# Two hybrid attention layers in float32 on one core: the broadcast of the forget logs through a scratch in device memory, issued by GpSimd

## The chip, the cores and the metric

The kernel runs on one core of a Trainium2 chip. A core has five engines that run their own instruction streams and meet at semaphores: TensorE (PE, matmuls; its weight loads are listed as PEld), VectorE (DVE), ScalarE (ACT), GpSimd (POOL) and SyncE (SP), which here does nothing but issue DMAs. Sixteen DMA engines move data between device memory and the on-chip memory SBUF, which has 128 partitions. Matmuls write to banks of a second on-chip memory, PSUM. The metric is device time of one execution in microseconds (us); lower is better.

## The reference

Two identical layers work on `x` of 512 tokens by 1024 channels. Each layer normalises and modulates `x`, projects it, and feeds three branches of four heads each: retention, gated linear attention (GLA) and forgetting attention ("fox"). The branches are gated, mixed and added to `x`; a gated feed-forward block with a short causal convolution follows. The branch that the change touches is this one:

```python
def forgetting_attention(q, k, v, f_logit):
    log_f = jax.nn.log_sigmoid(f_logit.astype(F32))
    cum = jnp.cumsum(log_f, axis=1).transpose(0, 2, 1)          # one row of 512 per head
    for blk in range(s // Q_BLOCK):                              # 128 queries at a time
        q0, q1 = blk * Q_BLOCK, (blk + 1) * Q_BLOCK
        logits = jnp.einsum('bihd,bjhd->bhij', q[:, q0:q1], k[:, :q1]) * d ** -0.5
        logits = logits + cum[:, :, q0:q1, None] - cum[:, :, None, :q1]
        ...
        p = jax.nn.softmax(jnp.where(mask, logits, -jnp.inf), axis=-1)
        outs.append(jnp.einsum('bhij,bjhe->bihe', p, v[:, :q1]))
```

In each logit the cumulated log of the query's position is added and that of the key's position subtracted. With queries on the partitions, the first is one number per partition, and the second is a row of 512 numbers that every partition needs.

## The kernel before

**Weights and matmuls.** All weights lie in device memory as `wall`, cut into 302 units of 128 x 1024 floats (512 KB) in the order of their use. A unit is loaded into a raw tile `wr` by SyncE (`dma_to`, L114; four buffers), copied by ScalarE into a rounded part `wh` (`prep_hi`, L122), and VectorE subtracts the two into the remainder `wl` (`prep_lo`, L131), which also frees the raw tile. Each product is made of three matmuls (high by high, high by low, low by high). `col_block` (L239 to L241) makes 128 channels by 512 tokens from one unit; `tok_group` (L534 to L536) makes token-major tiles from several units. `ahead` prepares units in advance of the one in use, four deep in the part that matters here.

**The order of the work.** The program order is written by hand, and every engine executes its own instructions in that order. SyncE's queue holds weight loads, tables and, before the change, the broadcasts. Beside the big matmuls, small pieces of the three branches ("items") are written as generators. `tick`, called within each block of matmuls, lets waiting items take a step: a step of kind "e" emits work of VectorE, ScalarE and GpSimd, a step of kind "p" emits matmuls, if enough of the three PSUM banks of the pool `psa` are free. An item that follows takes its turn from a queue with spacings written in the program.

**Around the change.** After the values of the fox branch (`fv`) come the projections of GLA's queries and keys; with the keys come the forget logits. `gk_evac` then queues `gates_item`, two `la_item` (the GLA decays), and sixteen `fox_item`, head by head and four query blocks each. Meanwhile TensorE makes GLA's values (`gv`, a `tok_group` of four units), then retention's queries (`rq`).

`gates_item` transposes the logits, forms the log-sigmoid, and VectorE's scan (L589) leaves `cum` with one head's 512 numbers in each of partitions 0 to 3. TensorE transposes it into `cumc` (L593), the per-query numbers. Then each head's row is broadcast into a tile `cumb` of 128 x 512 by a DMA (L597).

A `fox_item` multiplies queries and keys (`fs`, L649), after which VectorE forms the logits with `cumc` and `cumb` (L653), masks them and takes the maximum; ScalarE exponentiates (L658) and scales (L661); TensorE transposes the result (L665) and multiplies by the values (L675). An item may start only when its head's normalised queries and keys and the `cumb` tiles are there in the program's order. GpSimd, in this part of the program, has the multiplication in the normalisation of queries and keys (L492), before the gates, and the additions of the rotary embedding (L690), after GLA's values.

All [128, 512] tiles of float32 come from one pool of 59 slots, `cum` and `cumb` among them.

Of the kernel before, what the change touches and what calls it, by code (L numbers as in the profile page):

```python
# [7 lines left out]
F32 = mybir.dt.float32  # L8
# [17 lines left out]
S = 512  # L26
NH = 4
# [27 lines left out]
def tile_hybrid_layers(ctx: ExitStack, tc: tile.TileContext, xT, cvec, wall, wada, par, a2, cst, tabs, out):  # L55
# [5 lines left out]
    wh_p = ctx.enter_context(tc.tile_pool(name="wh", bufs=5))  # L61
    wl_p = ctx.enter_context(tc.tile_pool(name="wl", bufs=5))
    sm_p = ctx.enter_context(tc.tile_pool(name="sm", bufs=2))
    psm = ctx.enter_context(tc.tile_pool(name="psm", bufs=8 - NA, space=PS))
    psa = ctx.enter_context(tc.tile_pool(name="psa", bufs=NA, space=PS))

    V, A, G, T, Q = nc.vector, nc.scalar, nc.gpsimd, nc.tensor, nc.sync

    def slot(nm, dt=F32):
        return slots.tile([128, S], dt, tag="slot", name=nm)  # L70
# [6 lines left out]
    def free(n=1):  # L77
        live[0] -= n

    def ba(nm="ba"):  # L80
        live[0] += 1
        return psa.tile([128, S], F32, tag="a", name=nm)
# [3 lines left out]
    def cc(n):  # L86
        o, w = CC[n]
        return C[:, o:o + w]
# [3 lines left out]
    def pp(l, n, i=0, w=1):  # L92
        o, _ = PC[n]
        return P_l[l][:, o + i:o + i + w]
# [377 lines left out]
    def layer(l, nm, h):  # L472
# [80 lines left out]
        def gk_evac(b, o):  # L553
            if b == 0:
                R["gk"] = [slot("gk"), slot("gk")]
                R["sml"] = sm_p.tile([128, NB, 20], F32, tag="sml", name="sml")
            A.copy(R["gk"][b // 2][:, (b % 2) * 256:(b % 2) * 256 + 256], o[:, 0:256])
            V.tensor_copy(R["sml"][:, b, :], o[:, 256:276])
            if b == NB - 1:
                queue.append((gates_item(), 1))  # L560
                queue.append((la_item(0), 1))
                queue.append((la_item(1), 1))
                for hh in range(NH):
                    for ib in range(NB):
                        queue.append((fox_item(hh, ib), 1 + ib // 2))

        def gates_item():
            yield P1
            ps = ba("smT")
            for b in range(NB):  # L570
                T.transpose(ps[0:20, b * 128:b * 128 + 128], in_=R["sml"][:, b, :], identity=cc("ident"))
            yield E_
            gl = slot("glrT")
            V.memset(gl[0:32, :], 1.0)
            V.tensor_copy(gl[0:20, :], ps[0:20, :])
            free()
            e = slot("fe")
            m = slot("fm")
            fb = pp(l, "foxb")[0:4]
            A.activation(e[0:4], gl[0:4], AF.Abs, bias=fb)  # L580
            A.activation(e[0:4], e[0:4], AF.Exp, scale=-1.0)
            A.activation(e[0:4], e[0:4], AF.Ln, bias=cc("one")[0:4])
            V.tensor_scalar(m[0:4], gl[0:4], fb, 0.0, op0=ALU.add, op1=ALU.min)
            yield E_
            R["glrT"] = gl
            V.tensor_tensor(m[0:4], m[0:4], e[0:4], op=ALU.subtract)
            V.memset(e[0:4], 1.0)
            cum = slot("cum")
            V.tensor_tensor_scan(cum[0:4], e[0:4], m[0:4], 0.0, op0=ALU.mult, op1=ALU.add)  # L589
            yield P1  # L590
            pc = ba("cumc")
            for b in range(NB):
                T.transpose(pc[:, b * 4:b * 4 + 4], in_=cum[0:4, b * 128:b * 128 + 128],  # L593
                            identity=cc("ident")[0:4, 0:4])
            cb = [slot("cumb") for _ in range(NH)]
            for hh in range(NH):
                Q.dma_start(out=cb[hh], in_=cum[hh:hh + 1, None, :].to_broadcast([1, 128, S]))  # L597
            yield E_
            R["cumc"] = sm_p.tile([128, 16], F32, tag="cumc", name="cumc")
            V.tensor_copy(R["cumc"], pc[:, 0:16])  # L600
            free()
            R["cumb"] = cb
# [604 lines left out]
```

## Time and profile before

| | |
|---|---|
| Time, median of 3 runs | 1866.81 us (1865.39 to 1867.63) |
| Span of the profiled execution, first to last instruction | 1864.4 us (its time outside the span is not listed) |
| Matmuls | 8991 |
| DMA packets, data moved | 65395, 220.01 MB |
| DMA issues of the broadcasts | 8 (4 per layer), 256 KB written each |
| DMA issues of weight units | 302, 512 KB each |

How to read it: the profile lists each engine's busy time and its share of the span, then the span in 40 equal slices of 46.6 us, each with a digit for the busy tenth (9 is 90% or more). PEclk is the granted clock of TensorE in the same form. The chain of work goes back from the last instruction to what released it, step by step. A wait is put down to the event that came last. L numbers are lines of the kernel; `out<-in` gives the tiles' names; SPq is SyncE's queue. "us to landing" runs from a DMA's issue until its data have arrived.

### The profile page before, as it was taken

What the parts mean: (1) busy time and instruction counts of PE and PEld (TensorE: products, weight loads), DVE (VectorE), ACT (ScalarE), POOL (GpSimd) and SP (SyncE); (2) the same over time, 40 slices, a digit from 0 to 9 for tenths busy, and PEclk for the clock granted to TensorE, in tenths of its full rate; (3) what the DMA queues carried; (4) which work ended last, traced back from release to release, by engine and by line L of the source; (5) the groups of instructions that cost most, each with busy time, mean ns of one, the idle gap of its engine ahead of it and who ended that gap; (6) DMA issues with size and microseconds to landing.
All of it is one profiled execution on the core that took longest, in us unless ns stands there. A gap on an engine that the chain in (4) does not pass through costs nothing.

```text
span 1864.4 us, 22544 instructions
## 1 busy us (share of the span) xinstructions
PE 1805.6 (97%) x8991; PEld 1508.4 (81%) x8991; DVE 1002.1 (54%) x1515; ACT 672.2 (36%) x1124; POOL 85.4 (5%) x101
## 2 busy tenths in 40 slices
PE   9995999999999999999999869999999999999999
PEld 6874878888889888888898648788888898888887
DVE  7663754565665676764257347544434466444321
ACT  4662433332333443332148334333323244333210
POOL 3210100000000000000001001000000000000000
PEclk9997999999999999999999979999999999999999
DMA  9346222345552465554223542322222233322231
GB/s 335 126 55 92 69 91 90 125 158 192 169 181 86 152 236 181 191 193 158 79 69 124 38 98 69 102 91 69 90 95 98 79 102 102 100 93 94 71 121 55
DMA packets 65395, 220.01 MB, mean 118 GB/s; under 512 B 7263, under 2 KB 7689, under 8 KB 65290
## 3 DMA queue, kind: packets, MB, share of 16 engines
q1 hardware_dynamic: 65290, 218.57, 38.5%
q8 instruction: 71, 1.16, 0.3%
q14 instruction: 34, 0.28, 0.0%
HBM read 214.34 MB, written 2.10 MB: 116 GB/s over the span
## 4 chain that ended last, share of the span: by engine, by line
PE 92%; DMA 3%; DVE 2%; SPq 2%; ACT 1%; issue 0%; POOL 0%; DVEq 0%; ACTq 0%
PE bm L239 23%; PE bm L241 23%; PE bm L240 23%; PE bm L363 4%; PE ga L363 4%; PE bm L534 3%; DMA wr<-wall 3%; PE bm L535 2%; PE bm L536 2%; SPq L597 2%; PE ro L795 1%; PE rs L783 1%; PE fs L649 1%; PE fo L675 1%; PE go L761 0%; ACT wh L122 0%
## 5 line engine op out<-in xcount | busy, mean ns | idle before, releaser
L131 DVE TENSOR_TENSOR wl<-wr,wh 128x1024 fp32r<-128x1024 f32 x302 | 368.8, 1224 | 360.3 <-ACT wh L122 360.0
L239 PE MATMUL bm<-hhi,wh 128*128 128x512 f32 x1296 | 520.3, 401 | 0.0
L241 PE MATMUL bm<-hhi,wl 128*128 128x512 f32 x1296 | 505.5, 390 | 0.0
L240 PE MATMUL bm<-hlo,wh 128*128 128x512 f32 x1296 | 504.9, 390 | 0.0
L122 ACT CAST wh<-wr 128x1024 fp32r<-128x1024 f32 x302 | 314.5, 1047 | 358.5 <-PE bm L240 232.2
L239 PEld LDWEIGHTS bm<-hhi,wh 128*128 128x128 f32 x1296 | 243.4, 188 | 54.4 <-issue 4.2
L240 PEld LDWEIGHTS bm<-hlo,wh 128*128 128x128 f32 x1296 | 243.5, 188 | 53.0 <-issue 2.9
L241 PEld LDWEIGHTS bm<-hhi,wl 128*128 128x128 f32 x1296 | 243.2, 188 | 51.9
L239 PE MATMUL bm<-fah,wh 128*128 128x512 f32 (+1 forms) x374 | 141.0, 377 | 0.0
L240 PE MATMUL bm<-fal,wh 128*128 128x512 f32 (+1 forms) x374 | 140.8, 377 | 0.0
L241 PE MATMUL bm<-fah,wl 128*128 128x512 f32 (+1 forms) x374 | 140.8, 377 | 0.0
L534 PE MATMUL bm<-wh,hhi 128*128 128x512 f32 (+1 forms) x256 | 99.7, 389 | 0.0
L151 DVE SCALAR_TENSOR_TENSOR ar<-ar,cact 128x1024 f32<-128x1024 f32 x80 | 97.5, 1218 | 0.0
L535 PE MATMUL bm<-wl,hhi 128*128 128x512 f32 (+1 forms) x256 | 95.5, 373 | 0.0
L536 PE MATMUL bm<-wh,hlo 128*128 128x512 f32 (+1 forms) x256 | 95.1, 371 | 0.0
L240 PEld LDWEIGHTS bm<-fal,wh 128*128 128x128 f32 x374 | 70.3, 188 | 13.0
L241 PEld LDWEIGHTS bm<-fah,wl 128*128 128x128 f32 x374 | 70.3, 188 | 13.0
L239 PEld LDWEIGHTS bm<-fah,wh 128*128 128x128 f32 x374 | 70.3, 188 | 12.7
L904 DVE SCALAR_TENSOR_TENSOR x<-bm,mod,x 128x512 f32<-128x512 f32 (+1 forms) x39 | 25.5, 655 | 101.3 <-PE bm L241 101.3
L942 DVE TENSOR_TENSOR fu<-fu,bm 128x512 f32<-128x512 f32 x42 | 28.9, 688 | 69.6 <-PE bm L241 59.8
L867 ACT ACTIVATE mg<-bm,der 128x512 f32<-128x512 f32 x48 | 32.9, 685 | 82.4 <-PE bm L241 82.4
L941 ACT ACTIVATE fu<-fu 128x512 f32<-128x512 f32 x44 | 27.8, 632 | 93.9 <-DVE fu L939 93.9
(213 smaller groups left out, 2406.3 us busy)
## 6 DMA issues: line engine op xcount, KB each, us to landing
wr<-wall SPq DMA_DIRECT2D x302, 512.0 KB, 3.6
ar<-wada SPq DMA_DIRECT2D x80, 512.0 KB, 3.9
ad<-wada SPq DMA_DIRECT2D x32, 256.0 KB, 6.0
x<-xT SPq DMA_DIRECT2D x8, 256.0 KB, 4.2
cumb<-cum SPq DMA_DIRECT2D x8, 256.0 KB, 30.2
dec<-tabs SPq DMA_DIRECT2D x8, 256.0 KB, 4.3
out<-x SPq DMA_DIRECT2D x8, 256.0 KB, 2.1
cos<-tabs SPq DMA_DIRECT2D x2, 256.0 KB, 4.0
```

Source lines behind the costliest of these rows:

```text
L122: A.copy(hi, raw[i])
L131: V.tensor_tensor(lo, raw.pop(i), hi.bitcast(F32), op=ALU.subtract)
L151: V.scalar_tensor_tensor(out=r, in0=r, scalar=1.0, in1=cact, op0=ALU.mult, op1=ALU.mult, accum_out=mod[l][:, b:b + 1])
L239: T.matmul(o, lhsT=wh, rhs=ah, start=first, stop=False)
L240: T.matmul(o, lhsT=wh, rhs=al, start=False, stop=False)
L241: T.matmul(o, lhsT=wl, rhs=ah, start=False, stop=last)
L363: T.matmul(banks[f % GB][:, ts], lhsT=got[f // 8][wi][:, (f % 8) * 128:(f % 8) * 128 + 128], rhs=h[kc][hi][:, ts], start=kc == 0 and hf != ...
L534: T.matmul(o, lhsT=h[k][0][:, bs], rhs=wh[:, ws], start=k == 0, stop=False)
L535: T.matmul(o, lhsT=h[k][0][:, bs], rhs=wl[:, ws], start=False, stop=False)
L536: T.matmul(o, lhsT=h[k][1][:, bs], rhs=wh[:, ws], start=False, stop=k == KD - 1)
L597: Q.dma_start(out=cb[hh], in_=cum[hh:hh + 1, None, :].to_broadcast([1, 128, S]))
L867: A.activation(g, o, AF.Tanh, scale=0.5, bias=der[l][:, i * 8 + j:i * 8 + j + 1])
```

## The change

A pool of scratch tiles in device memory is added. In `gates_item`, GpSimd writes `cum` (four rows of 512 floats, 8 KB) into a scratch tile, and the four broadcasts read their row from the scratch in place of the SBUF tile. They are issued from GpSimd's queue in place of SyncE's. The destinations, the tiles' order and all other instructions stay as they were. The broadcasts depend on the write, so GpSimd issues them once the write has landed.

```diff
     sm_p = ctx.enter_context(tc.tile_pool(name="sm", bufs=2))
+    dr_p = ctx.enter_context(tc.tile_pool(name="dr", bufs=2, space=bass.MemoryType.DRAM))
     psm = ctx.enter_context(tc.tile_pool(name="psm", bufs=8 - NA, space=PS))
...
+            cd = dr_p.tile([NH, S], F32, tag="cumd", name="cumd")
+            G.dma_start(out=cd, in_=cum[0:NH])
             cb = [slot("cumb") for _ in range(NH)]
             for hh in range(NH):
-                Q.dma_start(out=cb[hh], in_=cum[hh:hh + 1, None, :].to_broadcast([1, 128, S]))
+                G.dma_start(out=cb[hh], in_=cd[hh:hh + 1, None, :].to_broadcast([1, 128, S]))
             yield E_
```

## The prediction

> **What bounds the kernel now.** I read the page first: engine shares, 40 slices, chain.
>
> ```profile
> span 1864.4 us, 22544 instructions
> PE 1805.6 (97%) x8991; PEld 1508.4 (81%) x8991; DVE 1002.1 (54%) x1515; ACT 672.2 (36%) x1124; POOL 85.4 (5%) x101
> PE   9995999999999999999999869999999999999999
> PEclk9997999999999999999999979999999999999999
> PE 92%; DMA 3%; DVE 2%; SPq 2%; ACT 1%; issue 0%; POOL 0%; DVEq 0%; ACTq 0%
> cumb<-cum SPq DMA_DIRECT2D x8, 256.0 KB, 30.2
> dec<-tabs SPq DMA_DIRECT2D x8, 256.0 KB, 4.3
> ad<-wada SPq DMA_DIRECT2D x32, 256.0 KB, 6.0
> out<-x SPq DMA_DIRECT2D x8, 256.0 KB, 2.1
> ```
>
> TensorE is the bound: it is busy 97% of the span. It is visibly idle in one place per layer only, the fourth slice and the 23rd and 24th, and its clock falls there too. The last rows point at a suspect: a 256 KB broadcast of `cum` takes a median 30.2 us to land, where 256 KB read from device memory take 4.3 us (`dec`) or 6.0 (`ad`).
>
> Next the windows view, cut at TensorE's own stops in layer 0 and then in layer 1. The columns are the stretch, its length, busy time of PE, PEld, DVE, ACT and POOL, granted clock, DMA share, GB/s.
>
> ```profile
> 113.00:130.87 17.87, 17.86 (x80) 13.82 (x79) 11.32 (x16) 8.82 (x13) 0.64 (x1) 1.00 0.35 11
> 130.87:135.46 4.59, 0.01 (x1) 0.01 (x1) 0.38 (x2) 0.00 (x0) 0.00 (x0) 0.89 0.92 27
> 135.46:141.17 5.71, 5.71 (x18) 4.84 (x18) 1.89 (x7) 2.33 (x8) 0.00 (x0) 0.50 0.92 27
> 141.17:147.30 6.13, 6.09 (x30) 4.72 (x28) 0.00 (x0) 0.00 (x0) 0.00 (x0) 0.99 0.90 27
> 147.30:166.60 19.30, 0.00 (x1) 0.00 (x1) 0.52 (x1) 1.60 (x3) 0.00 (x0) 0.61 0.90 102
> 166.60:172.30 5.70, 4.71 (x11) 2.87 (x12) 5.07 (x10) 1.66 (x6) 0.00 (x0) 0.53 0.55 190
> 1054.50:1057.57 3.07, 0.01 (x2) 0.00 (x1) 0.37 (x2) 0.00 (x0) 0.00 (x0) 1.00 0.90 27
> 1057.57:1062.00 4.43, 4.43 (x18) 3.73 (x19) 1.89 (x7) 2.33 (x8) 0.00 (x0) 0.72 0.90 27
> 1062.00:1068.20 6.20, 6.20 (x29) 4.76 (x27) 0.00 (x0) 0.00 (x0) 0.00 (x0) 0.93 0.91 27
> 1068.20:1088.76 20.56, 0.03 (x1) 0.00 (x1) 0.52 (x1) 1.59 (x3) 0.00 (x0) 0.62 0.90 97
> 1088.76:1094.40 5.64, 4.65 (x11) 2.87 (x12) 5.01 (x10) 1.66 (x6) 0.00 (x0) 0.57 0.54 192
> ```
>
> Each layer has two stops, a short one (4.6 and 3.1 us) and a long one (19.3 and 20.5 us), and half-speed matmuls after each. In all of it the DMA engines are 90% busy and move 27 GB/s.
>
> Third, the timelines of SyncE, VectorE, ScalarE and GpSimd around the stops, the chain, and the landing times of layer 0's four broadcasts (start, us, what).
>
> ```profile
> 95.49 0.33 SPq L114 DMA_DIRECT2D wr<-wall  x1
> 100.31 5.34 SPq L114 DMA_DIRECT2D wr<-wall  x2
> SPq L597 <- DVE cum L589: 17.3, 1, 17.3
> 122.98 17.81 SPq L597 DMA_DIRECT2D cumb<-cum  x4
> DMA to landing us min/median/max: 11.9/22.3/32.7
> 109.16 1.21 DVE L131 TENSOR_TENSOR wl<-wr,wh 128x1024 fp32r<-128x1024 f32 x1
> 114.20 1.22 DVE L131 TENSOR_TENSOR wl<-wr,wh 128x1024 fp32r<-128x1024 f32 x1 [2.10 <-ACT wh L122]
> 122.83 1.19 DVE L131 TENSOR_TENSOR wl<-wr,wh 128x1024 fp32r<-128x1024 f32 x1
> 126.43 1.21 DVE L131 TENSOR_TENSOR wl<-wr,wh 128x1024 fp32r<-128x1024 f32 x1
> 135.05 0.35 DVE L653 SCALAR_TENSOR_TENSOR fl<-fs,cumc,cumb 128x128 f32<-128x128 f32 x1 [7.41 <-DMA cumb<-cum]
> 138.30 0.79 ACT L661 ACTIVATE fl<-fl,fst 128x128 f32<-128x128 f32 x2
> 140.88 24.10 DMA wr<-wall
> 165.00 1.04 ACT L122 CAST wh<-wr 128x1024 fp32r<-128x1024 f32 x1 [25.92 <-DMA wr<-wall]
> 112.36 1.29 POOL L492 TENSOR_TENSOR qsq<-qsq,qv 128x512 f32<-128x512 f32 x1 [3.67 <-ACT qsq L491]
> 185.25 1.29 POOL L690 TENSOR_TENSOR rq<-rq,rt 128x512 f32<-128x512 f32 x1 [71.61 <-DVE fst L660]
> 1045.23 17.70 SPq L597 DMA_DIRECT2D cumb<-cum  x4
> 1048.68 1.21 DVE L131 TENSOR_TENSOR wl<-wr,wh 128x1024 fp32r<-128x1024 f32 x1
> ```
>
> The short stop: the first fox item (L653) waits for the first broadcast, issued at 122.98 and landed 11.9 us later; TensorE, which by the code holds three banks for such items and finds none free, waits behind it. The long stop: SyncE, which also loads the weights (L114), waits 17.3 us for `cum` and then needs 17.81 us to hand out four broadcasts, so no weight is issued from 105.65 to 140.88. The next one queues behind the broadcasts and lands 24.10 us after that; ScalarE, which executes in order, sits 25.92 us on its cast with the softmax work of the fox items behind it, and TensorE stands.
>
> **The change, part by part.** *The source.* Four broadcasts of 256 KB at 27 GB/s take 39 us of nearly all the DMA engines' time. The scratch replaces this source; the destinations stay. The trace has no row that reads one 2 KB row of device memory 128 times, so its landing is bounded: 4.3 us by `dec` (four issued together, same size) from below, 11.9 us, today's first broadcast, from above. It is nearest to the device-memory reads, and I take the slower of them, 6.0.
>
> On this the Trainium skill (SBUF — State Buffer, section Door 1: The DMA port swizzle) says that four partitions in a row share one DMA port of about 27.2 GB/s. The 27 GB/s above agrees with that. By the fit in the same page's section The DMA setup-cost knee, 2 us plus bytes at 436 GB/s, a broadcast from the scratch would take an estimated 2.6 us, and the sum below would have no residue: about 1808.6.
>
> *The write and its wait.* New: one 8 KB write per layer, four rows, and GpSimd must see it landed before it issues the broadcasts. Nearest landing: 2.1 us, a 256 KB store to device memory. No DMA of GpSimd is in the trace; an issue is bounded by 0.33 us, one of SyncE's (95.49), and 1.29 us, GpSimd's own 128x512 operation. I take 1.0 for each issue, nearer to GpSimd's row because the same engine does the work. Write leg 3.1, broadcast leg 7.0: first head ready 10.1 us after `cum`, against 11.9 today. Queued behind the waiting GpSimd instructions is only the rotary add (L690), which starts 72 us after the one before it; even pulled forward 30 us it is far behind. That idle GpSimd is the cover, and it costs nothing.
>
> *SyncE's queue.* It loses four DMA issues and the wait on `cum` per layer. Weights then go out when VectorE frees their buffers, at 110.4, 115.4, 124.0 and 127.6 (the ends of L131); three units are out before the broadcasts start at about 127, and land long before 140. The long stop goes: 19.30 − 0 in layer 0 and 20.53 in layer 1.
>
> *The short stop.* TensorE runs dry at 130.87 and resumes 0.4 us after the broadcast. In layer 0: 122.98 + 10.1 + 0.4 − 130.87 = 2.6 us left. In layer 1: 1045.23 + 10.1 + 0.4 − 1054.50 = 1.2 us. What is late next? After the resumption TensorE had 11.8 us of prepared work (135.46 to 147.30), some 9 at full clock, while ScalarE is through with the first fox items 4.0 us after the broadcast (139.09) and the next unit's cast and subtraction take 1.04 + 1.21, some 6.3 us in all: no new stop.
>
> *The clock.* In the windows after the stops busy time times the missing clock: 5.71×0.50 + 4.71×0.47 + 4.43×0.28 + 6.20×0.07 + 4.65×0.43 = 8.7 us. It returns with the stops; for the 2.6 us that remain in layer 0 I keep 1.0 (layer 1's 3.1 us stop cost 1.7).
>
> *Sum.* Idle lost now: layer 0, 4.58 + 0.04 + 19.30 + 0.99 = 24.9; layer 1, 3.06 + 20.53 + 0.99 = 24.6; with the clock 58.2. Residue 2.6 + 1.2 + 1.0 = 4.8. Gain 53.4. On the profiled span: 1864.4 − 53.4 = 1811.0; the page gives no other time of that execution, and the median of the runs shown, 1866.81, stands 2.4 above the span: **1813.4 us**. Bounds with all else equal: no residue, 1808.6; the first head landing in 11.9 us, the first rival.
>
> **Rivals.** *A. One row read 128 times is as slow as the SBUF partition.* For it: nothing in the trace reads a row twice. Against: every row of device memory lands in 4 to 6 us. The first head would come at 122.98 + 4.1 + 11.9 = 139.0, stops of 8.5 and 7.1 us, clock loss 5 as now after the short stops: 1808.6 + 20.6 = 1829, if the weights pass on their own queue. If they are also held until the broadcasts end (127 + 39 = 166), the three units gone out before bridge ScalarE's need from 143 to 158, at VectorE's pace of 5 us a unit (109.16 to 114.20); 8 us of stop and 2 of clock per layer come back: up to 1849.
>
> The Trainium skill (DMA: Bandwidth & Descriptors, section Issuing engines are not separate DMA queues) says that DMAs of all issuing engines share the same 16 DMA engines, and that another issuer saves only issue time. No run here shows it yet; by it the queue's move alone would leave the 39 us of occupied engines, and A is the case in which it would count.
>
> *B. GpSimd's issue is the slow step.* If GpSimd can't make its transfers while VectorE works, the write leaves when VectorE runs dry, at 127.64 (126.43 + 1.21) and 1049.89. Heads at 137.7 and 1060.0, stops of 7.2 and 5.9, clock 3.4: 1825. The same price comes from an issue of 5 us. For: VectorE is nearly busy there. Against: GpSimd is free.
>
> The Trainium skill (SBUF — State Buffer, section Who interferes with whom) holds that descriptor writing for GpSimd's DMAs is shut out while VectorE runs certain copies; the trace has no GpSimd DMA to show it.
>
> *C. Slower.* The row's reads are slower than the partition's and the weights wait for them. The place is the long stop, and the price is the time B for which four broadcasts occupy the engines. At B = 39 A's upper end still gains 18 us, 9 per layer, and each further us costs one per layer: it turns at B = 48, or 22 GB/s, and at B = 60 the time is 1866.8 + 2×12 = 1891. Speaks for it: 27 GB/s is already met from one place. Against: as for A, more strongly.
>
> *D. No change:* the weights wait for something else until 165. VectorE's buffer release is the candidate, but it comes at 127.64 at the latest: 1866.8.
>
> **How the numbers follow.** The forecast 0.74 (own range 1807 to 1822), A 0.11, B 0.09, C 0.04, D 0.02. The likeliest gives 1813. From 1806 to 1834 lie the forecast, B and the lower half of A, some 0.85. Only C is slower and D the same; within 0.2% (3.7 us, about what timing tells from no change) nothing else falls: faster 0.94, same 0.02, slower 0.04.
>
> **What would show it.** Right: the broadcasts land in 4 to 7 us; SyncE's weight loads appear between 106 and 123; the cast's wait of 25.92 is gone; the fourth and 23rd slices of PE read 9; the short stop is under 3 us. Wrong: broadcasts over 10 us with the engines near 90% busy (A, C); GpSimd's issues standing apart by several us, or starting only at 127.6 (B); a wait of ScalarE on weights over 5 us (A, C, D). The prediction fails first at the landing of one row read 128 times, the one term without a row of its own.

## The result, and the profile after

The changed kernel takes 1805.88 us (median of 4 runs, 1805.62 to 1807.32) against 1866.2 before (median of 4 runs, one more than in the table above): a ratio of 0.9676, 95% interval 0.9662 to 0.969, so 60.3 us less. The forecast was 1813 (1806 to 1834 with two of its rivals, 1807 to 1822 on its own). The direction and the causes of the stops held, the gain was underrated by 7 us, and the time lies 0.12 us below the wider range.

From the page of the changed kernel, the same parts as before (an added line in the file shifts its line numbers, by one at first and by three behind the change):

```profile
span 1805.5 us, 22557 instructions
PE 1796.0 (99%) x8991; PEld 1503.5 (83%) x8991; DVE 1001.8 (55%) x1515; ACT 672.4 (37%) x1124; POOL 91.0 (5%) x111
PE   9999999999999999999999999999999999999999
PEclk9999999999999999999999999999999999999999
PE 93%; DVE 4%; ACT 2%; issue 1%; DMA 0%; SPq 0%; POOL 0%; DVEq 0%; ACTq 0%
cumb<-cumd POOLq DMA_DIRECT2D x8, 256.0 KB, 4.6
```

Both holes in TensorE's row and its clock's dips are gone, SPq and DMA have left the chain, and a broadcast lands in 4.6 us in place of 30.2. The windows view around the change, cut where TensorE used to stop (columns as before):

```profile
113.27:131.14 17.87, 17.87 (x83) 14.18 (x82) 12.63 (x20) 9.08 (x14) 3.58 (x6) 1.00 0.37 113
131.14:150.00 18.86, 18.86 (x96) 15.54 (x97) 10.17 (x22) 10.47 (x26) 0.00 (x0) 1.00 0.27 92
1006.40:1024.30 17.90, 17.90 (x83) 14.20 (x82) 11.93 (x21) 9.36 (x15) 2.75 (x5) 1.00 0.44 137
1024.30:1064.00 39.70, 39.70 (x202) 32.72 (x201) 25.14 (x48) 18.96 (x41) 2.82 (x3) 1.00 0.21 71
```

TensorE is busy all the time at a clock of 1.00 in both layers: neither a long nor a short stop is left. The timelines of SyncE, GpSimd and VectorE in layer 0, and then the landing times of its four broadcasts from the tile's view:

```profile
100.57 45.87 SPq L115 DMA_DIRECT2D wr<-wall  x8
123.49 0.76 POOL L597 DMA_DIRECT2D cumd<-cum  x1 [9.59 <-DVE cum L590]
126.04 2.25 POOL L600 DMA_DIRECT2D cumb<-cumd  x4 [1.79 <-DMA cumd<-cum]
129.77 0.35 DVE L656 SCALAR_TENSOR_TENSOR fl<-fs,cumc,cumb 128x128 f32<-128x128 f32 x1 [1.87 <-DMA cumb<-cumd]
```

```profile
DMA to landing us min/median/max: 3.6/4.5/6.1
```

SyncE now sends weights throughout, among them two units at 110.66 and 115.73 us, where it stood still before. GpSimd writes at 123.49, issues the four broadcasts from 126.04, about 0.54 us each, and the first fox item starts at 129.77.

Where the time came from, layer by layer, is read off the scan that makes `cum`, an instruction both kernels have. VectorE's timeline before, then after:

```profile
121.69 1.21 DVE L589 TENSOR_TENSOR_SCAN cum<-fe,fm 4x512 f32<-4x512 f32 x1
1043.94 1.21 DVE L589 TENSOR_TENSOR_SCAN cum<-fe,fm 4x512 f32<-4x512 f32 x1
```

```profile
121.96 1.21 DVE L590 TENSOR_TENSOR_SCAN cum<-fe,fm 4x512 f32<-4x512 f32 x1
1013.76 1.21 DVE L590 TENSOR_TENSOR_SCAN cum<-fe,fm 4x512 f32<-4x512 f32 x1
```

From scan to scan, layer 0 shrank from 922.25 to 891.80, by 30.5 us; from the second scan to the end of the span, 820.5 became 791.7, by 28.7. The prediction's terms for idle time and clock give 24.9 + 5.1 = 30.0 and 24.6 + 3.7 = 28.2.

### The profile page after: what moved, and what is told of

It reads as the page before. It is cut to its first block, busy times and chain, and to the rows that moved or that the text cites. A ratio compares the mean times of both kernels' runs of the same rounds, so it can differ in the third digit from the quotient of the medians.

```text
span 1805.5 us, 22557 instructions
## 1 busy us (share of the span) xinstructions
PE 1796.0 (99%) x8991; PEld 1503.5 (83%) x8991; DVE 1001.8 (55%) x1515; ACT 672.4 (37%) x1124; POOL 91.0 (5%) x111
## 4 chain that ended last, share of the span: by engine, by line
PE 93%; DVE 4%; ACT 2%; issue 1%; DMA 0%; SPq 0%; POOL 0%; DVEq 0%; ACTq 0%
PE bm L240 23%; PE bm L242 23%; PE bm L241 23%; PE bm L364 4%; PE ga L364 4%; PE bm L535 3%; PE bm L536 3%; PE bm L537 3%; PE ro L798 1%; PE rs L786 1%; DVE fl L658 1%; ACT wh L123 1%; DVE wl L132 1%; DVE fst L659 1%; DVE fl L656 0%
```

## The experiments

The change has two parts, a new source and a new queue. Theory S puts the loss down to the rate at which one SBUF partition is read, theory K to SyncE's queue standing still.

**The source alone.**

```diff
-            G.dma_start(out=cd, in_=cum[0:NH])
+            Q.dma_start(out=cd, in_=cum[0:NH])
...
-                G.dma_start(out=cb[hh], in_=cd[hh:hh + 1, None, :].to_broadcast([1, 128, S]))
+                Q.dma_start(out=cb[hh], in_=cd[hh:hh + 1, None, :].to_broadcast([1, 128, S]))
```

> The changed kernel with the write to the scratch and the four broadcasts issued by SyncE in place of GpSimd: the new source alone. Theory S (the rate at which one SBUF partition is read is what cost the time): SyncE still waits for `cum` and now also for the write, but is free again near 128 us, and three weight units land by about 133, when ScalarE needs the first: 1806 to 1810 us, the cast's wait under 2 us. Theory K (what cost the time is that SyncE's queue stood still, and another queue is the cure): the weights are still held from 106 to 128, and a stop of some 5 us or more per layer stays: 1820 or more.

Measured: 1807.3 us, ratio 0.9678 (0.9664 to 0.9693), not to be told from the full change. SyncE's timeline, and the one wait of ScalarE for weights in layer 0:

```profile
101.13 5.34 SPq L115 DMA_DIRECT2D wr<-wall  x2
125.22 2.45 SPq L600 DMA_DIRECT2D cumb<-cumd  x4
127.76 88.17 SPq L115 DMA_DIRECT2D wr<-wall  x15
```

```profile
ACT wh L123 <- DMA wr<-wall: 1.4, 1, 1.4
```

Weights stand still from 106.5 to 127.76, but the broadcasts no longer block the engines, and the next unit comes 1.4 us late for ScalarE, without a stop of TensorE. This is what theory S expected. Theory K is refuted for the fast source: weights held from 106 to 128 us alone cost TensorE no stop.

**The queue alone.**

```diff
-                Q.dma_start(out=cb[hh], in_=cum[hh:hh + 1, None, :].to_broadcast([1, 128, S]))
+                G.dma_start(out=cb[hh], in_=cum[hh:hh + 1, None, :].to_broadcast([1, 128, S]))
```

> The kernel before with the four broadcasts issued by GpSimd in place of SyncE, still read from the SBUF partition: the new queue alone. Theory S: the first head lands about 12 us after its issue as before, both short stops stay (4.6 and 3.1 us, with clock about 12 us), and the DMA engines are some 90% busy at 27 GB/s for 39 us: 1818 or more, up to 1849 if the weights are held as well. Theory K: the weights pass on their own queue and the rest hides: 1806 to 1812.

Measured: 1824.54 us, ratio 0.9769 (0.9753 to 0.9785). TensorE's waits in layers 0 and 1, the landing times of layer 0's broadcasts, and that of the weight unit issued behind them at 128.57:

```profile
PE lan L632 <- DVE fl L653: 5.5, 1, 5.5
PE lan L632 <- DVE fl L653: 3.8, 1, 3.8
```

```profile
DMA to landing us min/median/max: 12.3/26.5/39.4
DMA to landing us min/median/max: 37.7/37.7/37.7
```

The short stops stay and the long ones go; the time is in theory S's range, and theory K is out. The unit landed only when the last broadcast did. That does not mean that no weights passed. Between 127 and 163 us GpSimd's queue q0 and SyncE's queue q1 moved (packets, MB, share of the 16 engines' time):

```profile
q0 software_dynamic: 284, 0.97, 92.3%
q1 hardware_dynamic: 250, 0.93, 6.3%
```

The two queues took turns, almost packet for packet, but a packet of a broadcast occupied its engine for far longer than a packet of weights. So not quite two units of weights passed in the whole time of the slow broadcasts. What then does the new queue gain?

**Weights ahead of the wait, on the old queue.** SyncE's order is changed in the kernel before, nothing else:

```diff
+            dma_to(state["lo"] + 4)
             cb = [slot("cumb") for _ in range(NH)]
```

> The kernel before, all on SyncE's queue and read from the SBUF partition, but SyncE issues the three weight units whose buffers come free meanwhile ahead of its wait for `cum`, where before they stood behind the wait and the broadcasts. Theory (what the new queue gains is only that three units are out before the slow transfers start, not that weights pass beside them): the long stop goes and the short stop stays, as in the kernel with the new queue alone, 1822 to 1828 us. Rival (a queue of its own lets weights pass): the unit behind the broadcasts is held as before and the long stop stays for the most part, 1845 to 1867.

Measured: 1825.0 us, ratio 0.9773 (0.9757 to 0.9789), the time of the new queue alone. SyncE's timeline and TensorE's waits in both layers:

```profile
99.90 24.05 SPq L114 DMA_DIRECT2D wr<-wall  x5
124.00 18.02 SPq L598 DMA_DIRECT2D cumb<-cum  x4
142.11 35.78 SPq L114 DMA_DIRECT2D wr<-wall  x6
```

```profile
PE lan L633 <- DVE fl L654: 6.3, 1, 6.3
PE lan L633 <- DVE fl L654: 4.6, 1, 4.6
```

Five units precede the broadcasts in place of two, and that alone removes the long stop, though SyncE is still held for 18 us. So the queue's worth here is that weights are not stuck behind the wait for `cum`. That some weights also pass beside the broadcasts on a queue of their own gained nothing more.

**Two queues, one or two places.** In the kernel before, SyncE issues heads 0 and 1 and GpSimd heads 2 and 3; the second kernel lets GpSimd read a copy in partitions 66 and 67.

```diff
+            cu2 = slot("cu2")
+            V.tensor_copy(cu2[64:68], cum[0:4])
...
-                Q.dma_start(out=cb[hh], in_=cum[hh:hh + 1, None, :].to_broadcast([1, 128, S]))
+                E, s, o = (Q, cum, 0) if hh < 2 else (G, cum, 0)    # second kernel: (G, cu2, 64)
+                E.dma_start(out=cb[hh], in_=s[o + hh:o + hh + 1, None, :].to_broadcast([1, 128, S]))
```

> The kernel before with its broadcasts split over two queues: heads 0 and 1 issued by SyncE, heads 2 and 3 by GpSimd, all read from partitions 0 to 3 of SBUF. (VectorE also copies `cum` to partitions 64 to 67, unread here; the next kernel reads it.) If the reads share one limit of 27 GB/s, two broadcasts at a time land in about 20 to 24 us each and all four end near 39 us after the first issue, as before. If each queue had 27 GB/s of its own, the heads would land in 12 and 22 us.

> As the kernel with two queues, but GpSimd's two broadcasts read partitions 66 and 67 in place of 2 and 3. If the limit lies with the place that is read (neighbouring partitions share it, far ones do not), both queues run side by side: heads 0 and 2 land in about 12 us and all four end near 20 us; 54 GB/s while it lasts. If it lies with the DMA engines or the total, nothing changes against the kernel with two queues.

Measured: 1867.95 us, ratio 1.0005 (0.9994 to 1.0015), and 1864.88, ratio 0.9985 (0.9975 to 0.9996). The first kernel in layer 0: the issues, the broadcasts' landing times (three of the four are recorded) and ScalarE's wait for weights.

```profile
121.55 1.19 SPq L600 DMA_DIRECT2D cumb<-cum  x2
121.78 1.34 POOL L600 DMA_DIRECT2D cumb<-cum  x2 [9.59 <-DVE cum L589]
```

```profile
DMA to landing us min/median/max: 12.1/26.8/40.0
```

```profile
ACT wh L122 <- DMA wr<-wall: 25.8, 1, 25.8
```

All four still end some 40 us after the issue, so 27 GB/s is one limit for both queues. The landings of single heads were not as expected: SyncE's first head landed in 12.1 us, as if alone, and GpSimd's first, issued 0.2 us later, took 26.8. The queues did not take turns from the start: from 122 to 134 us SyncE's moved 0.26 MB and GpSimd's 0.07, and only from 134 to 149 us were they even, with 0.18 and 0.21. SyncE hands out its two in 1.2 us, yet the weights behind them are as late as before.

With the second place the last landing, counted from SyncE's first issue, came after 39.1 us (162.1 − 123.0) in place of 41.0 (162.6 − 121.6), far from the 20 that two places side by side would give. But GpSimd's two were issued 3 us after SyncE's there, and while SyncE's first head was read, GpSimd's queue moved nothing. So the two places were hardly ever read at the same time, and the time of this kernel does not settle whether the limit is the place or the engines.

The records of single packets in the two traces say more. In the first kernel a 2 KB packet of SyncE's took 1.10 us when nearly all engines served its queue, and also when about half of them served GpSimd's, which reads the same place. In the second kernel, in the few moments when the engines were split over the two places, it took 0.60 us (9 packets), and a 4 KB packet of GpSimd's 0.91 us (2 packets) in place of 2.33. This points to the place that is read, from very few packets.

**How early the first head must come.** The scratch is copied twice more within device memory.

```diff
             G.dma_start(out=cd, in_=cum[0:NH])
+            for _ in range(2):
+                ce = dr_p.tile([NH, S], F32, tag="cumd", name="cume")
+                G.dma_start(out=ce, in_=cd)
+                cd = ce
```

> The changed kernel with the scratch copied twice more within device memory before the broadcasts: the first head comes later by two write legs, some 5.7 us by the 2.87 us that the first write takes. In the changed kernel the first head comes 0.96 us (layer 0) and 1.7 us (layer 1) before TensorE would run dry. Theory: beyond that slack each us of delay is a us of TensorE: stops of 4.7 and 4.0 us, with 3 to 4 us of clock, near 1818 us. Rival (the first head's time does not set TensorE's stop): 1806.

Measured: 1821.51 us, ratio 0.9751 (0.9737 to 0.9766). TensorE's waits in layers 0 and 1:

```profile
PE lan L639 <- DVE fl L660: 5.5, 1, 5.5
PE lan L639 <- DVE fl L660: 3.7, 1, 3.7
```

The first head came 13.0 and 12.6 us after `cum`, against 6.6 and 7.2 in the changed kernel: delays of 6.4 and 5.4. Less the slacks of 0.96 and 1.7 that is 5.4 and 3.7 us, which are the stops seen. The time is 3.5 us above the 1818 expected, because the clock cost more: it was 0.54 in the 5.2 us behind layer 0's stop and 0.52 in the 6.8 us behind layer 1's, which is 2.4 and 3.3 us. Stops and clock make 14.9 of the 15.6 us lost.

**Slow transfers that nobody waits for.** Behind the real broadcasts of the changed kernel, GpSimd issues further ones to device memory: four or two from the SBUF partition, or four from the scratch.

```diff
+            dd = dr_p.tile([NH, 128, S], F32, tag="dumd", name="dumd")
+            for hh in range(NH):            # range(2) in the second kernel
+                G.dma_start(out=dd[hh], in_=cum[hh:hh + 1, None, :].to_broadcast([1, 128, S]))   # cd in the third
```

> The changed kernel with four further broadcasts per layer from the SBUF partition, issued by GpSimd behind the real ones and written to device memory, where nobody reads them: the slow transfers without anyone who waits for them. If the weights on SyncE's queue pass beside them (packets in turn), three units ahead are enough: 1806 to 1812 us, weight landings up from 3.5 to about 11 us meanwhile. If the occupied engines hold the weights until the slow transfers end, some 8 us of stop and 2 of clock per layer: 1822 or more.

Measured: 1830.31 us, ratio 0.9797 (0.9783 to 0.9812). The time is in the second range, but the cause is in neither expectation: ScalarE never waits for weights around it; TensorE stands 9.6 us in each layer, and the profile names no cause. Its timeline in layer 0, and then the DMA queues (packets, MB, share of 16 engines) in the stretches 112 to 135, 135 to 160 and 160 to 170 us. Of these the lines of GpSimd's queue q0 and of the fetch queue q8 are shown where there are any, and for the second stretch that of SyncE's queue q1:

```profile
161.75 0.39 PE L240 MATMUL bm<-hhi,wh 128*128 128x512 f32 x1
171.77 0.80 PE L241 MATMUL bm<-hlo,wh 128*128 128x512 f32 x1 [9.63 <-issue]
```

```profile
q0 software_dynamic: 392, 1.22, 26.2%
...
q0 software_dynamic: 197, 0.66, 94.0%
q1 hardware_dynamic: 7, 0.01, 0.1%
...
q0 software_dynamic: 83, 0.23, 72.0%
...
q8 instruction: 1, 0.02, 0.6%
```

Here SyncE's queue moved almost nothing beside the slow transfers, though a weight unit had been issued at 136.79 us; in the kernel with the queue alone it had taken turns. Why is open.

Queue q8 moves 16 KB pieces of instructions, 71 in all. For TensorE's 17982 matmuls and weight loads that is one piece for some 253, so the queue is taken to be TensorE's. None arrives between 106.2 and 169.5 us; in the changed kernel one arrives between 130 and 136. TensorE restarts when the slow transfers are through and a piece has come.

> The changed kernel with two, not four, further broadcasts per layer from the SBUF partition to device memory that nobody reads. With four, TensorE stood 9.6 us per layer for no cause that the profile names, while the fetch of its instructions, which uses the same DMA engines, came only when the slow transfers were through. Theory (fetch held back): two of them are through near 148 us, before TensorE runs out of fetched instructions at 162: no stop, 1806 to 1809 us. Rival (each slow transfer costs its share): half of the 24 us that four cost, about 1818.

Measured: 1806.87 us, ratio 0.9675 (0.966 to 0.9689): no stop. Half the slow transfers cost nothing, so the cost is not in proportion to their number. The next piece of instructions came at 147.9 us, as the theory has it.

> The changed kernel with four further broadcasts per layer to device memory that nobody reads, read from the scratch in place of the SBUF partition: the same number of transfers and bytes as in the kernel that took 1830 us, without the slow source. Theory (the slow source is what holds the engines): 1806 to 1808 us. Rival (the number of transfers or their destination): 1818 or more.

Measured: 1806.33 us, ratio 0.9675 (0.9658 to 0.9691): the same bytes from the scratch cost nothing. Landing times in layer 0 of the two from the partition, then of the four from the scratch:

```profile
DMA to landing us min/median/max: 12.9/16.9/20.8
```

```profile
DMA to landing us min/median/max: 6.7/7.3/8.0
```

Destination and rows are alike; the source makes the difference.

That the late fetch is what stopped TensorE fits all three kernels; no run isolates it. Counts from the traces speak for it. With four slow transfers TensorE executed 542 matmuls and weight loads in layer 0, and 534 in layer 1, between the last piece and its stop. In the kernel with the queue alone the pieces were just as late (none from 106.2 to 165.0 us), but because of the short stops it had executed only 481 and 521 by then, and it did not stop. With two slow transfers it was 419 and 422.

## Why the prediction was right or wrong

*The two stops and their causes: right.* The source alone removes both, and weights sent ahead of the wait remove the long one, as the account of its cause requires. One reading was loose: the engines did not move 27 GB/s in all of the stretches shown, since the rows of the long stops have 102 and 97, with the weights that poured in at their ends. No term rests on it. The 58.2 us of idle and clock are borne out within half a microsecond per layer (30.5 and 28.7 against 30.0 and 28.2).

*The step that failed is the size of the broadcast leg.* It was taken at 7.0 us (1.0 for the issue, 6.0 for the landing by `ad`). From the issue at 126.04 to the first fox item at 129.77 it measured 3.7, and 4.6 in layer 1 (1017.61 to 1022.21). Two things were wrong in it. The landing was 3.6 us, nearer to the lower bound, 4.3 by `dec`, the row of four transfers of the same size, issued together. And the 1.0 was counted twice, because landing times run from the issue and hold it already. With 4.3 and no issue beside it the sum has no residue.

The write leg was 2.9 us (123.17 to 126.04) against 3.1, a hit that is partly luck: the issue began 0.3 us after `cum`, the write landed in 2.0, and the broadcasts began 0.6 later. The first head is ready 6.6 us after `cum` in place of 10.1, before TensorE runs dry, so the residue of 4.8 us is zero. The copies within device memory show that this residue would have been real: past the slack each us of delay is a us of stop, and clock besides.

*The rest of the miss.* Without the residue the forecast would have been 1808.6, still 2.7 us above the median. Of these, 0.7 lie in the span (1864.4 − 58.2 = 1806.2 against 1805.5). Another 0.6 lie in the time outside it, taken at 2.4 from the median of the runs and the span of one, where the profiled execution after has 1.8. And 1.4 come from the runs' spread: the profiled execution, 1807.32, is the slowest of its four. The range's low end, 1806, left too little room below the bound for these.

*Rival A did not come; its price can be tested in part.* One row read 128 times is served as fast as other rows. The kernel with the queue alone has A's slow broadcasts without its write leg of 4.1 us per layer. Less these 8.2 us, A's prices are 1821 if weights pass and 1841 if they are held. It took 1824.5: weights passed in turn, a unit was late by 34 us, and yet no long stop came. The units sent ahead bridge more than the 15 us reckoned at VectorE's pace of 5 us a unit: there ScalarE's casts behind the broadcasts start at 140.82, 153.87, 159.40 and 167.93, and the late unit, the last of these, lands at 166.3.

*B did not come.* GpSimd issued at 123.49 and 126.04 while VectorE worked from 123.10 to 127.9, and the four issues took 2.25 us; in the kernel with two more copies, where VectorE sat idle, 2.18. B's other form, an issue of 5 us, was given too low a price: by the prediction's terms both legs hold an issue of 1.0, so the head would have come 8 us later and not 4.7 (127.64 − 122.98). The Trainium skill's section Who interferes with whom (SBUF — State Buffer) ties the lockout to certain copies; VectorE's work here (subtractions, and reads of PSUM) shows none. *C* fell with A, and *D* with ScalarE's wait for weights, which is gone.

*The shared engines.* The Trainium skill (DMA: Bandwidth & Descriptors, section Issuing engines are not separate DMA queues) was set against the queue's move, and the trace agrees: on its own queue a weight unit took 37.7 us. The Trainium skill's section Queues, rings and completion order, on the same page, has each engine take turns between queues packet by packet. The kernel with the queue alone agrees, with 284 and 250 packets of the two queues between 127 and 163 us. With four transfers to device memory in the background the packets were 197 and 7 from 135 to 160 us, which differs, and the measurement stands.

The parts do not add: the source alone gains 59.4 us, the queue alone 42.2, both 60.3. The long stop needs both the slow source and weights stuck behind the wait, so either part removes it; the short stop yields only to the source.

## What to carry to other kernels

Look at a transfer's source as well as its size: 256 KB out of one SBUF partition kept all DMA engines 90% busy at 27 GB/s, and a round trip of 2.9 us through device memory was far cheaper. Such a transfer slowed what shared the engines with it, weights on another queue and, as far as the traces show, instructions; here a queue of its own helped only by freeing what was stuck behind its wait. When a term is bounded by rows, take the row most alike in form, check what its time already includes, and let the range reach past the bound by the spread of the runs.

## What the hardware showed that was not expected

An in-order queue's wait and the engines' occupation are two separate delays. Moving the broadcasts to GpSimd's queue and moving three weight loads ahead of the wait gave the same time (1824.5 and 1825.0 us). A weight unit on another queue still landed only with the last slow broadcast. It was not shut out: the queues took turns, and the slow broadcasts' packets took 92.3% of the engines' time for 0.97 MB, the weights' 6.3% for 0.93 MB.

Instruction fetches travel on the same DMA engines. With four slow transfers in the background no piece came for 63 us (106.2 to 169.5), and TensorE stopped for 9.6 us with nothing in the profile's waits but "issue"; with two it did not stop. That the one caused the other is supported by the counts of instructions executed until the stop, not shown by a run of its own.
